# Local attention moved beside later projections, and the second score product over 128 partitions

## The chip, the cores and the metric

The kernel runs on one core of one Trainium2 chip. Its time is the device time of one execution in microseconds (us); three runs of the kernel before gave 2787.1, 2791.96 and 2795.49, median 2791.96. The trace comes from a further, profiled execution. The engines are TensorE (PE: matrix products; PEld: its weight loads), VectorE (DVE), ScalarE (ACT), GpSimd (POOL) and SyncE (SP, which here issues most transfers).

## The reference

A network of three blocks on 512 tokens of width 1024. The change lies in the first two, which are called layer 0 and layer 1 here. Such a layer takes tokens `x` (512) and context `xc` (256), normalizes and modulates them, projects them with `w_in`, and mixes four branches of 256 columns:

```
h  = rms_norm(x, n1) * (1 + sc1) + sh1;   hc likewise        # mods = silu(c) @ ada_w + ada_b
a_b, a_c, a_h, b_v, b_g, c_q, c_k, c_v, d_q, d_k, d_v = split_proj(h @ w_in)
ya = a_b * dwconv(a_c * a_h, conv_a)                         # 3 taps
yb = silu(layer_norm(dwconv(b_v * sigmoid(b_g), conv_b) + bias))      # 31 taps
yc = window_attention(rope(c_q), rope(c_k), c_v, kc_c, vc_c, sink)    # +-128 tokens, and the context
yd = global_attention(rope(rms_norm(d_q)), rope(rms_norm(d_k)), d_v, kc_d, vc_d)   # all 512, and the context
x  = x + g1 * (concat(ya, yb, yc, yd) @ w_out)
x  = x + g2 * expert_choice_ffn(rms_norm(x, n2) ...)          # 16 experts
```

There are 4 query heads of 64 columns in each attention and 2 key heads. In layer 0 the context goes through all of this too, in layer 1 it gives keys and values alone. A third block (gated delta rule, dilated attention, a wide feed-forward) follows.

## The kernel before, in words

Activations lie transposed, 128 channels on the partitions and tokens along the free axis, so a projection of 128 columns of `w_in` is one *unit*: 8 blocks of weights, each multiplied three times (`dense`, L418). Weights and activations are split in a high and a low part of a fast 32-bit type; high by high, high by low and low by high give full precision. A product over the 512 tokens writes PSUM tile `px` (L462), one over the 256 context tokens a second tile of the same name (L464, `pc` in the code). A unit's weights come by a transfer into one of five `raw` tiles, ACT makes the high part `wh` (L438), POOL the low part `wl` (L439); the transfer is asked for three units ahead. After a unit its eviction `ev` reads `px`: for queries and keys it applies the rotation `rope` (DVE L664, L666, L667 and POOL L665) and splits the result in high and low parts (L643 to L647), which small POOL transfers copy into the other half of the partitions.

The two long convolutions of layer 0 and 1 (`conv31`, L760) are 31 DVE instructions per 128 channels, one per tap, each adding into the same tile (L769, L772).

Attention (`att_gen`, `attend` L526) goes through *items*: one block of 128 queries and one pair of heads. A head's scores are one or two `s` tiles (own block with neighbours or all 512 tokens; the context). Each `s` tile is made of two products (L542): the query tile holds its high part on 64 partitions and its low part on the other 64, and meets the high part of the keys on both halves; the second product takes the 64 high query partitions alone and the low part of the keys. Then come the maximum (DVE L495 or L499), the exponential (ACT L510), the scaling by the sum (DVE L522, L523), transposes on PE (`pt`, L554), their copies (`PT`, ACT L557 for one head and DVE L559 for the other), and the product with the values (`y`, L572). There are two `s` tiles, one `pt`, one `y`, and one tile `misc` that modulation, head norms and convolution statistics share.

`ada_gen` makes the modulation: 16 of its blocks (L315, L324) run in layer 0 beside this work, each with four transfers of 512 KB into the same `raw` tiles.

What is interleaved with what is written in three `run_all` calls in program order, each a weave of generators with weights: (1) the units of branch b and 8 modulation steps; (2) the units of c and d, 16 modulation steps and all of `conv31`; (3) the six units of branch a, all of attention, and the rest of the modulation. In layer 1, which has no modulation to make, queries of c and d stand between the units of b already, and the long convolution starts after the eighth unit. Within this order a list scheduler of the framework may move an instruction ahead of others; each engine then runs its own list in order.

Of the kernel before, what the change touches and what calls it, by code (L numbers as in the profile page):

```python
# [134 lines left out]
def main_kernel(ctx, tc, I, out, stop=None, dbg=None, manual=False):  # L135
# [132 lines left out]
    for j in range(2):  # L268
        pre0[j] = raw_tile().rearrange("p (k c) -> p k c", k=8)
        SY.dma_start(pre0[j], I["w_in"][0, :, 1024 + 128 * j:1152 + 128 * j].rearrange("(k p) c -> p k c", p=128))  # L270
# [67 lines left out]
    if True:  # L338
# [79 lines left out]
        def dense(units, hh, hl, dw, dps, la=3, pre={}):  # L418
# [23 lines left out]
            for i in range(la):  # L442
                load(i)
            split(0)
            fresh = True
            for i, u in enumerate(units):
                ev, nt = u[1], u[2]
                k0, nk = u[3:5] if len(u) > 3 else (0, 8)
                load(i + la)
# [76 lines left out]
        def attend(ap, aps, groups, pw=768):  # L526
# [19 lines left out]
            def turn(i, g):  # L546
# [3 lines left out]
                for a in range(0, nt, 4):  # L550
# [4 lines left out]
                    pb = ap.tile([128, 512], F32, name="PT", bufs=4 if pw > 512 else 3)  # L555
# [34 lines left out]
        def layer(l):  # L590
# [6 lines left out]
            with (es_l0 if has else ExitStack()) as es, ExitStack() as er:  # L597
# [3 lines left out]
                sqp = pool(es, "sqp", 5)  # L601
# [20 lines left out]
                kC = dp.tile([128, 3, 768], F32R)  # L622
                kD = dp.tile([128, 3, 768], F32R)
# [10 lines left out]
                nrq = dp.tile([128, 2, 6, 2], F32)  # L634

# [13 lines left out]
                def put_q(dst, j, o, n, src, scale=None):  # L649
                    c = slice(o, o + n)  # L650
                    t = sqp.tile([128, 512], F32R, name="ql", bufs=2)
# [4 lines left out]
                def put_k(dst, o, n, src, scale=None):  # L656
                    c = slice(o, o + n)
                    split_to(dst[H0, 0, c], dst[H1, 1, c], dst[H0, 2, c], dst[H1, 2, c], src, scale)
                    G.dma_start(dst[H1, 0, c], dst[H0, 0, c])
                    G.dma_start(dst[H0, 1, c], dst[H1, 1, c])  # L660
# [197 lines left out]
                def qunit(n, ev, j):  # L858
                    return (colload2(w_in, c0[n] + 64 * j, c0[n] + 128 + 64 * j), ev, NT)

                u_kv = [unit("c_k", ev_rope(partial(put_k, kC)), 768), unit("d_k", ev_dk, 768),
                        unit("c_v", ev_v(vC), 768), unit("d_v", ev_v(vD), 768)]
                u_q = [qunit("c_q", ev_rope(partial(put_q, qC, j)), j) for j in range(2)] + \
                      [qunit("d_q", ev_dq(j), j) for j in range(2)]
# [4 lines left out]
                def terms(qt, kt, kv, g, n, a, b):  # L869
                    pr = slice(64 * kv, 64 * kv + 64)  # L870
                    q = qt[:, g, kv, n * 128:(n + 1) * 128]
                    return [(q, kt[:, kv, a:b]), (q[pr, :], kt[pr, 2, a:b])]

                def att_gen():
                    groups = []
                    for kv in range(2):
# [36 lines left out]
                        groups.append((hs, tuple(range(4)), yT[:, 6 + kv, 0:512], 512))  # L913
                        if has:
                            groups.append((hs, (4, 5), yT[:, 6 + kv, 512:768], 256))
# [963 lines left out]
```

## Time and profile before

| | |
|---|---|
| median of three runs | 2791.96 us |
| profiled execution, its own time | 2776.78 us |
| its span in the trace | 2774.0 us |
| PE busy | 2585.3 us, 93% |
| DVE, ACT, POOL busy | 1178.4, 876.3, 590.1 us |
| mean granted clock of PE | 0.974 |

Times in the trace count from the start of the span. Layer 0's projections and attention stand from 48 to 438 us, its output projection to 502, its experts to 1164; layer 1's from 1164 to 1439, output projection to 1470, experts to 1990; the third block fills the rest. A stretch in which PE is busy nearly throughout is bound by PE, and there only less work or shorter work on PE helps; one in which it is not is read by what ended its waits.

### The profile page before, as it was taken

What the parts mean: (1) busy time and instruction counts of PE and PEld (TensorE: products, weight loads), DVE (VectorE), ACT (ScalarE), POOL (GpSimd) and SP (SyncE); (2) the same over time, 40 slices, a digit from 0 to 9 for tenths busy, and PEclk for the clock granted to TensorE, in tenths of its full rate; (3) what the DMA queues carried; (4) which work ended last, traced back from release to release, by engine and by line L of the source; (5) the groups of instructions that cost most, each with busy time, mean ns of one, the idle gap of its engine ahead of it and who ended that gap; (6) DMA issues with size and microseconds to landing.
All of it is one profiled execution on the core that took longest, in us unless ns stands there. A gap on an engine that the chain in (4) does not pass through costs nothing.

```text
span 2774.0 us, 41538 instructions
## 1 busy us (share of the span) xinstructions
PE 2585.3 (93%) x16527; PEld 1530.4 (55%) x16527; DVE 1178.4 (42%) x2466; ACT 876.3 (32%) x1812; POOL 590.1 (21%) x495
## 2 busy tenths in 40 slices
PE   7989999799999999888997998889899999999998
PEld 3556677434444444466664321223377787888876
DVE  4684574412323233587653110212375555444411
ACT  4225443211111211334442211111354425444422
POOL 3243002000000000273111000000233232444443
PEclk9999999899999999899998999999899999999999
DMA  8655206599998988231047999999721102333331
GB/s 286 221 165 160 77 24 225 175 344 399 341 389 321 387 314 341 65 80 54 24 153 282 391 400 398 400 399 409 259 63 47 31 16 61 92 99 99 92 87 65
DMA packets 318327, 570.99 MB, mean 206 GB/s; under 512 B 36320, under 2 KB 187415, under 8 KB 317495
## 3 DMA queue, kind: packets, MB, share of 16 engines
q1 hardware_dynamic: 311143, 552.01, 55.4%
q0 software_dynamic: 6848, 16.27, 2.4%
q8 instruction: 130, 2.13, 0.3%
q14 instruction: 62, 0.51, 0.1%
q10 hardware_dynamic: 144, 0.08, 0.0%
HBM read 553.60 MB, written 10.49 MB: 203 GB/s over the span
## 4 chain that ended last, share of the span: by engine, by line
PE 70%; DMA 13%; DVE 8%; issue 1%; ACT 1%; POOL 1%; SPq 0%; ACTq 0%; DVEq 0%; POOLq 0%
PE px L462 19%; PE ax L1200 4%; PE ux L1200 4%; PE yx L1200 4%; PE s L542 3%; DMA rawA<-in_w_down_dram 3%; DVE yT L772 3%; PE y L572 3%; PE px L464 2%; PE g L462 2%; PE pt L554 2%; PE ac L1205 2%; PE tr L1313 2%; PE uc L1205 2%; PE yc L1205 2%; DMA rawA<-in_w_up_dram 2%
## 5 line engine op out<-in xcount | busy, mean ns | idle before, releaser
L439 POOL TENSOR_TENSOR wl<-raw,wh 128x512 fp32r<-128x512 f32 (+1 forms) x312 | 406.1, 1304 | 1046.1 <-ACT wh L438 755.3
L438 ACT ACTIVATE wh<-raw 128x512 fp32r<-128x512 f32 (+1 forms) x312 | 193.4, 625 | 469.5 <-PE px L462 209.7
L462 PE MATMUL px<-hh,wh 128*128 128x512 f32 x768 | 315.0, 412 | 8.0 <-DVE xT L1316 1.8
L462 PE MATMUL px<-hh,wl 128*128 128x512 f32 x768 | 315.9, 412 | 4.1 <-POOL wl L439 4.1
L462 PE MATMUL px<-hl,wh 128*128 128x512 f32 x768 | 315.6, 411 | 2.2 <-DVE hl L1004 1.9
L1284 DVE SCALAR_TENSOR_TENSOR Yx<-yx,gcol,Yx 64x512 fp32r<-64x512 f32 x64 | 48.0, 750 | 502.2 <-ACT Yx L1283 502.2
L1166 POOL DMA_INDIRECT xg<-hd,gidx x32 | 29.2, 914 | 845.6 <-PE tr L1178 787.3
L462 PEld LDWEIGHTS px<-hh,wh 128*128 128x128 f32 x768 | 148.2, 193 | 51.3 <-issue 12.4
L462 PEld LDWEIGHTS px<-hl,wh 128*128 128x128 f32 x768 | 148.4, 193 | 41.6 <-issue 11.3
L462 PEld LDWEIGHTS px<-hh,wl 128*128 128x128 f32 x768 | 148.8, 194 | 40.7 <-POOL wl L439 6.9
L1182 ACT ACTIVATE xt<-tr,mod,a 128x64 f32<-128x64 f32 x256 | 86.1, 405 | 197.3 <-PE tr L1178 193.2
L772 DVE SCALAR_TENSOR_TENSOR yT<-ub,cols,yT 128x512 f32<-128x512 f32 (+1 forms) x180 | 147.2, 862 | 1.2
L1283 ACT ACTIVATE Yx<-yx,gcol 64x512 fp32r<-64x512 f32 x64 | 43.6, 682 | 318.6 <-PE yx L1200 158.6
L1228 ACT ACTIVATE sa<-ax 128x512 f32<-128x512 f32 x32 | 19.1, 597 | 353.6 <-PE ax L1200 240.5
L1200 PE MATMUL ax<-rawA,xt 128*32 128x512 f32 x856 | 122.3, 603 | 0.0
L1200 PE MATMUL ux<-rawA,xt 128*32 128x512 f32 x800 | 119.2, 595 | 0.0
L1194 PE MATMUL ux<-rawA,xt 128*64 128x512 f32 x328 | 87.3, 611 | 7.7 <-DMA rawA<-in_w_up_dram 7.4
L1194 PE MATMUL yx<-rawA,hT 128*64 128x512 f32 x316 | 81.5, 621 | 13.0 <-DMA rawA<-in_w_down_dram 12.1
L1313 PE MATMUL tr<-oh,Yx 128*128 128x512 f32 x256 | 79.9, 440 | 11.3 <-ACT Yx L1283 8.1
L554 PE MATMUL pt<-tab,P 128*128 128x128 f32 x448 | 87.0, 289 | 3.0 <-ACT PT L557 1.5
L1194 PE MATMUL ax<-rawA,xt 128*64 128x512 f32 x316 | 77.3, 610 | 6.9 <-DMA rawA<-in_w_gate_dram 6.4
L464 PE MATMUL px<-hh,wh 128*128 128x256 f32 x240 | 73.2, 305 | 7.0 <-ACT sq L673 7.0
(573 smaller groups left out, 4907.5 us busy)
## 6 DMA issues: line engine op xcount, KB each, us to landing
rawA<-in_w_gate_dram SPq DMA_DIRECT2D x186, 512.0 KB, 9.4
rawA<-in_w_up_dram SPq DMA_DIRECT2D x182, 512.0 KB, 10.2
rawA<-in_w_down_dram SPq DMA_DIRECT2D x151, 512.0 KB, 10.4
raw<-in_ada_w_dram SPq DMA_DIRECT2D x80, 512.0 KB, 4.9
raw<-in_w_down_dram SPq DMA_DIRECT2D x74, 512.0 KB, 7.3
raw<-in_w_gate_dram SPq DMA_DIRECT2D x62, 512.0 KB, 10.1
raw<-in_w_in_dram SPq DMA_DIRECT2D x56, 512.0 KB, 4.9
raw<-in_w_up_dram SPq DMA_DIRECT2D x55, 512.0 KB, 6.5
```

The source lines that it names most:

```text
L438: A.activation(wh[:, :n], raw[i][:, a:a + n], AF.Copy)
L439: G.tensor_tensor(wl[:, :n], raw[i][:, a:a + n], wh[:, :n].bitcast(F32), op=OP.subtract)
L462: T.matmul(px, lhsT=w[:, k % 4, :], rhs=h[:, k0 + k, 0:512], start=st, stop=sp_)
L464: T.matmul(pc, lhsT=w[:, k % 4, :], rhs=h[:, k0 + k, 512:nt], start=st, stop=sp_)
L542: T.matmul(s[:, :w], lhsT=q, rhs=k, start=(a == 0), stop=(a == len(mm) - 1))
L554: T.transpose(pt[:, (t - a) * 128:(t - a + 1) * 128], P[:, t * 128:(t + 1) * 128], ident)
L772: V.scalar_tensor_tensor(acc[:, j, o:o + n], src, w, acc[:, j, o:o + n], op0=OP.mult, op1=OP.add)
L1182: A.activation(xt[:, kk, 0:64], p[:, k * NX:k * NX + 64], AF.Identity, bias=M[l][:, 24 + kk, 0:1], scale=a2[:, kk, 0:1])
L1194: T.matmul(px[64 * g:64 * g + 64, :], lhsT=lx(u), rhs=w[:, 512 * hf:512 * hf + 512], start=first, stop=last)
L1200: T.matmul(px[32 * g:32 * g + 32, :], lhsT=lx(u)[:, 32 * (g % 2):32 * (g % 2) + 32], rhs=w[:, 512 * hf:512 * hf + 512], start=first, stop= ...
L1205: T.matmul(pc[32 * g:32 * g + 32, :], lhsT=lc(u), rhs=w[:, 256 * q:256 * q + 256], start=first, stop=last)
L1313: T.matmul(p, lhsT=Y["x", pr][:, hl_, hf, c * 128:(c + 1) * 128], rhs=ohs[pr][hf], start=(n == 0), stop=(n == 2 * len(prs) - 1))
```

## The change

1. Each score tile's second product reads all 128 partitions: the keys' tile gets a fourth plane, so that the low parts of a key head lie on both halves too, and the whole query tile meets them (L542 is L553 afterwards). The small transfers after a key's split carry two planes each. The low query part loses its own two buffers and lies in a tile of the shared group `sq` until it is copied.
2. The units come as c, b, d, a in place of b, (c and d), a. The attention's items come as all of c, then all of d.
3. There are four weaves in place of three: the units of c alone; those of b with 28 of the 120 attention steps (18 of 80 in layer 1) and 8 modulation steps; those of d with as many and a part of `conv31` (16 of 42 steps, 8 of 21 in layer 1); those of a with the rest of all.
4. In layer 0 four units' weights are asked for at first, and after that the next unit's alone (`ahead=4`). The first two units' weights, loaded at entry, are now those of `c_k` and the first `c_q`.
5. The transposed probabilities use one group of tiles for the first 512 columns (`PT`) and another for the rest (`PU`), two buffers each, in place of four of one. `sqp` has 7 buffers in layer 1, 5 in layer 0 as before.

```diff
-        def dense(units, hh, hl, dw, dps, la=3, pre={}):
+        def dense(units, hh, hl, dw, dps, la=3, pre={}, ahead=None):
...
-                load(i + la)
+                load_to(i + la + 1 if ahead is None or i + la < ahead else max(ahead, i + 2))
                 split(i + 1)
...
-                    pb = ap.tile([128, 512], F32, name="PT", bufs=4 if pw > 512 else 3)
+                    pb = ap.tile([128, 512 if a == 0 else pw - 512], F32, name="PT" if a == 0 else "PU",
+                                 bufs=2 if pw > 512 else 3)
...
-                sqp = pool(es, "sqp", 5)
+                sqp = pool(es, "sqp", 5 if has else 7)
...
-                kC = dp.tile([128, 3, 768], F32R)
-                kD = dp.tile([128, 3, 768], F32R)
+                kC = dp.tile([128, 4, 768], F32R)
+                kD = dp.tile([128, 4, 768], F32R)
...
-                    t = sqp.tile([128, 512], F32R, name="ql", bufs=2)
+                    t = sqp.tile([128, 512], F32, name="sq")
...
                 def put_k(dst, o, n, src, scale=None):
                     c = slice(o, o + n)
-                    split_to(dst[H0, 0, c], dst[H1, 1, c], dst[H0, 2, c], dst[H1, 2, c], src, scale)
-                    G.dma_start(dst[H1, 0, c], dst[H0, 0, c])
-                    G.dma_start(dst[H0, 1, c], dst[H1, 1, c])
+                    split_to(dst[H0, 0, c], dst[H1, 1, c], dst[H0, 2, c], dst[H1, 3, c], src, scale)
+                    G.dma_start(dst[H1, 0:4:2, c], dst[H0, 0:4:2, c])
+                    G.dma_start(dst[H0, 1:4:2, c], dst[H1, 1:4:2, c])
...
                 def terms(qt, kt, kv, g, n, a, b):
-                    pr = slice(64 * kv, 64 * kv + 64)
                     q = qt[:, g, kv, n * 128:(n + 1) * 128]
-                    return [(q, kt[:, kv, a:b]), (q[pr, :], kt[pr, 2, a:b])]
+                    return [(q, kt[:, kv, a:b]), (q, kt[:, 2 + kv, a:b])]
...
-                mix = [u for p in zip(u_b, u_q) for u in p]
-                gd = dense((u_b + u_kv + u_q if has else mix + u_kv) + u_a, hh, hl, dw, psp, pre=pre0 if has else {})
-                n1 = 4 if has else 8
-                run_all((dense_part(gd, n1 * 3), n1 * 3), (steps(ga, 8), 8))
-                run_all((dense_part(gd, (12 - n1) * 3), 36 - n1 * 3), (steps(ga, 16), 16), (conv31(), 42 if has else 21))
-                run_all((gd, 18), (att_gen(), 120 if has else 80), (ga, 20))
+                gd = dense(u_c + u_b + u_d + u_a, hh, hl, dw, psp, pre=pre0 if has else {}, ahead=4 if has else None)
+                at, cv = att_gen(), conv31()
+                w1, w2, w3 = (28, 28, 64) if has else (18, 18, 44)
+                run_all((dense_part(gd, 12), 12))
+                run_all((dense_part(gd, 12), 12), (steps(at, w1), w1), (steps(ga, 8), 8))
+                c1 = 16 if has else 8
+                run_all((dense_part(gd, 12), 12), (steps(at, w2), w2), (steps(ga, 8), 8), (steps(cv, c1), c1))
+                run_all((gd, 18), (at, w3), (ga, 16), (cv, (42 if has else 21) - c1))
```

How the order on the engines moves is shown at three places. First PE's list in layer 1, at the second transposes of the key norm of d (`misc<-tab,sq`, L709 before and L722 after). Before:

```order
L464 MATMUL px<-hh,wl 128x256
L462 MATMUL px<-hh,wh 128x512
L709 MATMUL misc<-tab,sq 128x128 x2
L464 MATMUL px<-hh,wh 128x256
L462 MATMUL px<-hl,wh 128x512
L464 MATMUL px<-hl,wh 128x256
```

And at the same transposes in the changed kernel, where `s`, `pt` and `y` are attention's:

```order
L473 MATMUL px<-hh,wl 128x512
L722 MATMUL misc<-tab,sq 128x128 x2
L473 MATMUL px<-hh,wh 128x512
L473 MATMUL px<-hl,wh 128x512
L473 MATMUL px<-hh,wl 128x512
L553 MATMUL s<-kC,qC 128x384 x2
L553 MATMUL s<-kC,qC 128x256 x2
L565 MATMUL pt<-tab,P 128x128 x4
L584 MATMUL y<-PT,vC 64x128
L473 MATMUL px<-hh,wh 128x512
```

The window attention now stands between the products of the projections of d; before, none stood there, and all of it came after them.

Second DVE's list in layer 1, in the key norm of d (L698 to L710), where the taps of the long convolution (L772, L785 afterwards) stand. Before:

```order
L772 SCALAR_TENSOR_TENSOR yT<-ub,cols,yT 128x512 x11
L698 RECIPROCAL hr<-hsd 128x12
L772 SCALAR_TENSOR_TENSOR yT<-ub,cols,yT 128x512
L705 COPY sq<-hr 128x512
L772 SCALAR_TENSOR_TENSOR yT<-ub,cols,yT 128x512 x3
L710 TENSOR_TENSOR sq<-sq,misc 128x512
```

After, a piece of the list with taps and the steps of the softmax (L506 to L534):

```order
L782 TENSOR_SCALAR yT<-ub,cols 128x512
L785 SCALAR_TENSOR_TENSOR yT<-ub,cols,yT 128x512 x2
L525 SCALAR_TENSOR_TENSOR sms<-sms 128x1
L785 SCALAR_TENSOR_TENSOR yT<-ub,cols,yT 128x512
L533 RECIPROCAL sms<-sms 128x1
L506 ISA P,sms<-s,tabl 128x256
L506 ISA sms 128x1
L534 TENSOR_SCALAR P<-P,sms 128x512
L510 TENSOR_REDUCE sms<-s 128x1
L785 SCALAR_TENSOR_TENSOR yT<-ub,cols,yT 128x512
```

The runs of taps are shorter, and between them stand softmax steps, for which PE's next score tile waits.

Third ACT's list in layer 0, at the sigmoid of branch b (L748, L750; L761, L763 afterwards), where tables of functions are loaded. Before:

```order
L438 ACTIVATE wh<-raw 128x512
L750 ACT_TABLE_LOAD
L750 ACTIVATE yT<-px 128x256
L748 ACTIVATE yT<-px 128x512
L438 ACTIVATE wh<-raw 128x512 x2
L320 ACTIVATE sq<-misc 128x512
```

After:

```order
L521 ACTIVATE P,sms<-s,sms 128x256
L761 ACT_TABLE_LOAD
L761 ACTIVATE yT<-px 128x512
L763 ACTIVATE yT<-px 128x256
L442 ACTIVATE wh<-raw 128x512
L569 ACTIVATE PT<-pt 128x512
L518 ACT_TABLE_LOAD
L518 ACTIVATE sms<-sinkb,sms 128x1
L521 ACTIVATE P,sms<-P,sms 128x384
```

The exponential of attention now stands on both sides of the sigmoid, so its table is loaded again behind each. In the whole list of ACT there are 53 table loads before and 72 after.

## Rows read from the trace of the kernel before

**Rows 1.** The page: span, busy time and share, chain by line, transfers of `w_in`

```profile
span 2774.0 us, 41538 instructions
PE 2585.3 (93%) x16527; PEld 1530.4 (55%) x16527; DVE 1178.4 (42%) x2466; ACT 876.3 (32%) x1812; POOL 590.1 (21%) x495
...
raw<-in_w_in_dram SPq DMA_DIRECT2D x56, 512.0 KB, 4.9
```

**Rows 2.** Busy time by stretch (columns in the first line)

```profile
core 0: us, PE busy (x) PEld busy (x) DVE busy (x) ACT busy (x) POOL busy (x), PEclk, DMA share, GB/s
48.00:107.00 59.00, 55.00 (x267) 33.47 (x266) 28.84 (x52) 18.19 (x31) 20.39 (x17) 0.97 0.68 223
107.00:232.00 125.00, 110.72 (x606) 76.69 (x604) 96.81 (x168) 37.99 (x67) 52.19 (x49) 0.97 0.58 168
232.00:438.00 206.00, 205.48 (x1230) 133.40 (x1228) 128.79 (x397) 97.82 (x266) 28.52 (x26) 0.99 0.27 82
...
1164.00:1202.00 38.00, 36.25 (x145) 28.21 (x145) 27.13 (x42) 19.75 (x36) 21.79 (x18) 0.93 0.36 90
1202.00:1278.00 76.00, 58.75 (x280) 47.88 (x279) 73.06 (x87) 21.09 (x39) 51.56 (x43) 0.87 0.27 68
1278.00:1439.00 161.00, 155.54 (x897) 104.69 (x897) 104.45 (x294) 81.08 (x213) 22.39 (x18) 0.99 0.13 43
```

**Rows 3.** Chain that ended last, 1199 to 1285 us (start, us, what)

```profile
by line: DVE yT L772 67.4%; issue 5.6%; PE px L462 4.3%; DVE sq L667 3.1%; DVE sq L666 2.5%; DVE sq L664 2.5%; POOL sq L665 2.4%; DVE yT L769 2.3%; PE px L464 2.0%; PE misc L709 1.5%; DVE nrq L719 1.4%; DVE rq L718 1.4%; PE misc L781 1.3%; 
...
1201.26 1.68 DVE yT L772
...
1244.34 11.38 DVE yT L772 x11
```

**Rows 4.** PE's instructions in order (start, us, ...); score pairs and projections

```profile
293.16 1.43 PE L542 MATMUL s<-kD,qD 128*128 128x512 f32 x4
294.53 0.44 PE L554 MATMUL pt<-tab,P 128*128 128x128 f32 x2
...
355.11 0.59 PE L542 MATMUL s<-kC,qC 128*128 128x256 f32 x2
355.62 0.39 PE L464 MATMUL px<-hh,wh 128*128 128x256 f32 x1
...
357.42 0.39 PE L462 MATMUL px<-hh,wl 128*128 128x512 f32 x1
357.65 0.28 PE L464 MATMUL px<-hh,wl 128*128 128x256 f32 x1
357.77 0.70 PE L542 MATMUL s<-kC,qC 128*128 128x384 f32 x2
358.40 0.65 PE L554 MATMUL pt<-tab,P 128*128 128x128 f32 x4
```

**Rows 5.** PE's weight loads in order, the same stretch; idle time in brackets

```profile
357.65 0.19 PEld L542 LDWEIGHTS s<-kC,qC 128*128 128x128 f32 x1
358.03 0.18 PEld L542 LDWEIGHTS s<-kC,qC 64*128 64x128 f32 x1 [0.19 <-issue]
358.40 0.42 PEld L554 LDWEIGHTS pt<-tab,P 128*128 128x128 f32 x4 [0.19 <-issue]
```

**Rows 6.** The instructions of L542: duration min/median/max, shapes and counts

```profile
L542 PE MATMUL s<-kC,qC x144: 275/381/681, 229.9 to 1389.8; 128*128 128x256 f32 x56, 64*128 64x256 f32 x56, 128*128 128x384 f32 x16, 64*128 64x384 f32 x16
L542 PE MATMUL s<-kD,qD x144: 275/385/792, 293.2 to 1426.0; 128*128 128x256 f32 x40, 64*128 64x256 f32 x40, 128*128 128x512 f32 x32, 64*128 64x512 f32 x32
```

**Rows 7.** The taps of L772: duration min/median/max, shapes and counts

```profile
L772 DVE SCALAR_TENSOR_TENSOR yT<-ub,cols,yT x180: 464/739/1860, 95.6 to 1282.6; 128x512 f32<-128x512 f32 x120, 128x256 f32<-128x256 f32 x60
```

**Rows 8.** Groups of ACT, 232 to 438 us: busy, mean ns, idle before

```profile
L507 ACT ACT_TABLE_LOAD x2 | 2.6, 1283 | 0.0
```

**Rows 9.** Transfers of L654 (a query's low part), issue to landing

```profile
DMA to landing us min/median/max: 1.9/2.8/7.3
```

More of the change, by code (lines that the diff above doesn't have):

```diff
@@ L267, in main_kernel @@
     pre0 = {}
-    for j in range(2):
-        pre0[j] = raw_tile().rearrange("p (k c) -> p k c", k=8)
-        SY.dma_start(pre0[j], I["w_in"][0, :, 1024 + 128 * j:1152 + 128 * j].rearrange("(k p) c -> p k c", p=128))
+    pre0[0] = raw_tile().rearrange("p (k c) -> p k c", k=8)
+    SY.dma_start(pre0[0], I["w_in"][0, :, 1536:1664].rearrange("(k p) c -> p k c", p=128))
+    pre0[1] = raw_tile().rearrange("p (k c) -> p k c", k=8)
+    for h in range(2):
+        SY.dma_start(pre0[1][:, :, 64 * h:64 * h + 64],
+                     I["w_in"][0, :, 1280 + 128 * h:1344 + 128 * h].rearrange("(k p) c -> p k c", p=128))
     ada_load(0, 3, ada0[:, 3])
@@ L440, in split, with load_to @@
                         hi[i].append((wh, wl))
-            for i in range(la):
-                load(i)
+            loaded = 0
+            def load_to(n):
+                nonlocal loaded
+                while loaded < n:
+                    load(loaded)
+                    loaded += 1
+            load_to(la)
             split(0)
@@ L859, in qunit @@
                     return (colload2(w_in, c0[n] + 64 * j, c0[n] + 128 + 64 * j), ev, NT)
[L861 to L864, printed above, removed]
+                u_c = [unit("c_k", ev_rope(partial(put_k, kC)), 768)] + \
+                      [qunit("c_q", ev_rope(partial(put_q, qC, j)), j) for j in range(2)] + [unit("c_v", ev_v(vC), 768)]
+                u_d = [unit("d_k", ev_dk, 768)] + [qunit("d_q", ev_dq(j), j) for j in range(2)] + \
+                      [unit("d_v", ev_v(vD), 768)]
                 u_b = [unit("b_g", ev_bg(j), j=j) for j in range(2)] + [unit("b_v", ev_bv(j), j=j) for j in range(2)]
@@ L869, in terms @@
                 def terms(qt, kt, kv, g, n, a, b):
-                    pr = slice(64 * kv, 64 * kv + 64)
                     q = qt[:, g, kv, n * 128:(n + 1) * 128]
-                    return [(q, kt[:, kv, a:b]), (q[pr, :], kt[pr, 2, a:b])]
+                    return [(q, kt[:, kv, a:b]), (q, kt[:, 2 + kv, a:b])]
                 def att_gen():
-                    groups = []
+                    groups, late = [], []
                     for kv in range(2):
@@ L912, in att_gen @@
                                            nscale=lambda n, kv=kv, g=g: nrq[:, g, n, kv:kv + 1], sink=None, nsink=None))
-                        groups.append((hs, tuple(range(4)), yT[:, 6 + kv, 0:512], 512))
+                        late.append((hs, tuple(range(4)), yT[:, 6 + kv, 0:512], 512))
                         if has:
-                            groups.append((hs, (4, 5), yT[:, 6 + kv, 512:768], 256))
-                    yield from attend(ap, psp, groups)
+                            late.append((hs, (4, 5), yT[:, 6 + kv, 512:768], 256))
+                    yield from attend(ap, psp, groups + late)
                 def rest():
```

## The prediction

> **What bounds the kernel now.** I read the page first, then the busy time by stretch over the two layers' mixing, then the chain of waits in the stretch where PE is least busy, then PE's instructions one by one where attention runs. On the page PE is busy 93% of the span and DVE, the next, 42% [rows 1]: what is worth anything has to shorten PE's work or close PE's gaps. The stretches show which of the two holds where [rows 2]. In layer 0 from 48 to 232 us and in layer 1 from 1202 to 1278 us PE has gaps; in the attention stretches (232 to 438, 1278 to 1439) it has nearly none, and DVE is busy only 63 and 65% there. So each layer has two unlike parts: one where DVE decides, followed by one where PE decides. In the first the chain of waits says why: between 1199 and 1285 us two thirds of it are the taps of the long convolution, in one run of 11 for 11.38 us [rows 3], and a projection's eviction or a head norm stands behind them on DVE. In the second PE's list is attention and projections, and there I looked at what one matmul costs from start to start, since durations overlap.
>
> Those starts are the main finding. A projection product of 512 columns is followed by the next after 357.65 - 357.42 = 0.23 us, one of 256 columns after 357.77 - 357.65 = 0.12 us [rows 4]. A pair of score products of 256 columns takes 355.62 - 355.11 = 0.51 us, where two at 0.12 would be 0.24; a pair of 384 takes 358.40 - 357.77 = 0.63 us, where I estimate 2 x 0.175 = 0.35 between the two sizes; two pairs, of 512 and of 256, take 294.53 - 293.16 = 1.37 us, where 0.70 would do [rows 4]. The weight loads show where the rest goes: the first one, over 128 partitions, is done ahead of time, the 64-partition one starts only 0.38 us after it with 0.19 us of idle time that nothing else explains, and the load behind it, again over 128 partitions, has the same 0.19 us [rows 5].
>
> **The change, part by part.** *The second product over 128 partitions.* A pair becomes two products of the shape that projections have. If that is the cause, a 256 pair gains 0.27 us, a 384 pair 0.28, a 512 and a 256 pair together 0.67. By the counts there are 144 pairs: 96 of 256, 16 of 384, 32 of 512 [rows 6]. 32 of the 256 pairs go with the 512 ones: 32 x 0.67 = 21.4; the other 64 x 0.27 = 17.3; 16 x 0.28 = 4.5; together 43 us. All of it lies on PE in the stretches in which PE is bound. It could be less by what remains at the end of a pair, when transposes or a value product follow; the low end is half, 21, since half of the excess stands behind the 64-partition product. I take 43, since the rows show both halves.
>
> The Trainium skill ("TensorE: Matmul & The Clock Gate", section LDWEIGHTS) states that a weight load over 32 partitions takes as long as one over 128, and its closing table says the same of a small-K matmul by itself. The durations here agree (0.18 and 0.19 us) [rows 5], the starts do not: by that rule the 43 us would be 0. The change from one shape to the other is what its table has no line for.
>
> *The wider key planes.* `put_k` keeps its two transfers with twice the bytes, ACT and POOL split as much as before: 0. The low query part now takes one of the five `sq` tiles until its copy has landed, 2.8 us at the median [rows 9]; a query eviction then holds four of five. If the next of the four query evictions in layer 0 waits for that in full, it is 4 x 2.8 = 11 us; at the other end nothing, or a gain where the two buffers of before were the shortage. I take 0: a unit of 24 products of each size lasts 24 x 0.35 = 8.4 us, longer than the landing.
>
> *The long convolution among attention.* This closes gaps of PE. In layer 0 the stretch from 107 to 232 has 125 - 110.7 = 14.3 us of them, in layer 1 that from 1202 to 1278 has 76 - 58.75 = 17.3 [rows 2], together 31.6. PE then gets attention's products to fill them with, and the order shows that it does. DVE's own work is also less there: the taps have a median of 0.74 us but a largest of 1.86 [rows 7], and single ones in the chain take 1.68 [rows 3] while POOL is busy 51.6 of 76 us [rows 2]. The taps of the last weave meet a POOL that only splits weights, so DVE should not become longer. The cover for this is that PE's work stays above DVE's. In layer 0 DVE has 28.8 + 96.8 + 128.8 = 254 us in 390, PE 371 less 24 (80 of the 144 pairs are layer 0's); in layer 1 DVE 204.6 and PE 250.5 less 19 [rows 2]. So PE still leads in both, by 90 and by 27 us; in layer 1 it is close. The granted clock of 0.87 there [rows 2] says that part of PE's work ran at the lower level of 1.2 GHz after gaps; were it all at 2.4 GHz, up to 13% of 76 us = 10 us would come back. I take none of it, since part lies in gaps already counted.
>
> *What it adds.* ACT gets 19 more table loads of 1.283 us [rows 8], 24 us. They lie on an engine that is busy 97.8 of 206 us [rows 2], but each stands between scores and their exponential, and PE has only two score tiles. At one end they are all covered (0), at the other all on the path (24); I take the half, 12, by ACT's half-busy time. The shallower request for weights in layer 0 would cost at most 14 units x 4.9 us = 69 if a transfer [rows 1] were never covered, and nothing if always; with one unit asked for when the one before it begins, and units of at least 8.4 us, I take 0. The first weave of layer 0 loses its modulation, and with it its modulation transfers; what it loses there stands again in later weaves: 0. Split `PT` and `PU` tiles give each head as many as before: 0. Evictions of c in the first weave bring POOL work (rotation, splitting, 12 small transfers) beside the weight splits; POOL was busy 20.4 of 59 us there [rows 2], so 0.
>
> The sum: 43 + 14.3 + 17.3 - 12 = 62.6 us less. Made against the profiled execution, 2776.8 - 63 = 2714. The median of the runs shown lies 15 us above that execution, so the same difference from it gives 2792 - 63 = 2729 us.
>
> **The rivals.** *Shape does not matter.* If the excess of a pair comes from something that the change leaves alone (the switch to a new score tile, the same weights twice), 43 falls away: 31.6 - 12 = 20 us less, 2772. For it speaks that the loads themselves take equally long; against it that the idle time stands at exactly the two loads where the shape changes [rows 5], while projections switch tiles without it [rows 4]. The rule of the Trainium skill's TensorE page named above gives this outcome.
>
> *DVE takes over in the last weave.* With taps and softmax on one list, a score tile's maximum waits behind a run of taps, and PE with it. If the gaps of the two stretches are only moved, the 31.6 us stay: 43 - 12 = 31 less, 2761. Layer 1, with its 27 us of difference between the engines, is where it would be; for it speaks DVE's 73 of 76 us today [rows 2], against it that the runs of taps become shorter in the order.
>
> *All of it goes well.* No table load is felt and the clock comes back too: 43 + 31.6 + 10 = 85 less, 2707.
>
> *Slower: lock step through two score tiles.* Each of the 144 pairs needs its maximum before PE may write the pair after the next. If on average each waits for one tap behind POOL's use (1.68 us [rows 3]) in place of none, that is 144 x 1.68 = 242 us, less 74.6 gained: 2792 + 167 = 2959. It decides from 74.6 / 144 = 0.52 us a pair. A table load in front of every fourth exponential as well would add to it. Against it: today's pairs wait on DVE's side for PE, not the reverse, and PE's list has projections between pairs, so a short wait is filled. A milder form, 0.7 us a pair, gives 100 - 75 = 26 slower, 2818.
>
> That the change doesn't do what it says I leave out: the order shows attention among the units of b and d.
>
> **How the numbers follow.** Forecast (with the neighbours up to 15 us off) 0.50; all goes well 0.14; DVE takes over 0.18; shape does not matter 0.10; slower 0.08. Faster by over 0.3% (8 us, about what a measurement of this kernel can tell from no change, since its three runs lie 8.4 us apart) takes in the first three and nearly all of the fourth: 0.89; within 0.3% 0.04, slower 0.07. The range leaves out the slower rival and the far ends of the first two: 2695 to 2772. Its upper end is the outcome in which the shape is worth nothing, its lower end goes a little past the case in which all goes well, for a gain at the clock in layer 0 as well.
>
> **What would show it.** In the changed kernel's trace a pair of 256 should take about 0.24 us from start to start, of 512 about 0.46, no load of L553 should have 64 partitions, and the "issue" idle time at these loads should be gone. The attention stretches should be shorter by PE's work, with PE still without gaps. Taps should appear all over the second half of each layer with a mean near 0.74 us for 512 columns. PE's gaps in the former convolution stretches should be gone, and PE's clock near 1.0 there. ACT should show 19 more table loads in the two layers. Layer 0 should end its attention some 35 us earlier, layer 1 take some 30 us less from first projection to output projection; the experts and the third block should be as long as before. I would be wrong if pairs keep their 0.5 us, if PE waits for DVE's maxima over some 10 us in a layer, or if layer 0's first weave stalls on `sq` tiles or weights.

## The result, and the profile after

The changed kernel takes 2694.65 us (median of four runs, 2689.85 to 2696.23) against 2792.29 for the kernel before beside it: a ratio of 0.9649, 95% interval 0.963 to 0.9668. Two later comparisons gave 0.9682 (0.965 to 0.9715) and 0.9648 (0.9634 to 0.9661). The forecast was 2729, so the gain of some 95 us (98, and 86 and 100 by the medians of the later two) was half as large again as the 63 forecast, and 2694.65 lies just outside the range, by 0.35 us. Since the kernel before varies more than the changed one (its medians beside the runs of this study went from 2779 to 2792), I profiled both again; rows below named "before" are of that second execution (span 2784.5 us), and those of the changed kernel too (2692.0 us; its first had 2692.1).

The page of the changed kernel, for [rows 1]: TensorE has 77 us less to do than in the first profile of before, and is still what bounds the kernel.

```profile
span 2692.0 us, 41575 instructions
PE 2508.4 (93%) x16527; PEld 1523.7 (57%) x16527; DVE 1159.8 (43%) x2466; ACT 900.6 (33%) x1831; POOL 589.6 (22%) x495
```

To see where the time went, I cut from each trace the same work: from a layer's first projection to the last unit of its output projection, first layer 0, then layer 1. Before:

```profile
core 0: us, PE busy (x) PEld busy (x) DVE busy (x) ACT busy (x) POOL busy (x), PEclk, DMA share, GB/s
47.10:496.70 449.60, 430.73 (x2420) 291.69 (x2421) 271.87 (x649) 168.86 (x390) 116.76 (x104) 0.98 0.46 146
1165.20:1473.60 308.40, 286.31 (x1423) 207.31 (x1424) 212.76 (x430) 130.83 (x300) 109.46 (x87) 0.91 0.26 83
```

After:

```profile
46.90:445.80 398.90, 381.90 (x2420) 291.18 (x2421) 268.30 (x649) 181.25 (x401) 120.72 (x104) 0.96 0.54 167
1109.90:1378.50 268.60, 249.82 (x1423) 194.10 (x1424) 198.87 (x430) 141.66 (x308) 104.25 (x87) 0.95 0.31 98
```

PE has the same number of instructions in both, so this is like against like: 758.0 us became 667.5, 90.5 less, and the spans differ by 92.5. TensorE's gaps (length less PE busy) went from 41.0 to 35.8 only; its busy time fell by 85. I sorted that busy time by the starts of PE's instructions: score products went from 96.5 to 53.8 us (43 less, as forecast), modulation's products in layer 0 from 54.7 to 34.7 (20 less, not forecast), everything else by 23, of which 16 in layer 1, where the same instructions ran at a mean granted clock of 0.95 in place of 0.91. The other 7 are layer 0's, where the clock was not higher (0.96 after 0.98); what they are stays open.

How much of this is gaps and clock depends on the execution. In the first execution of before the same work took 746.4 us:

```profile
47.70:494.00 446.30, 427.48 (x2420) 289.79 (x2421) 271.65 (x649) 168.78 (x390) 116.62 (x104) 0.98 0.47 147
1163.70:1463.80 300.10, 275.40 (x1423) 199.32 (x1424) 213.61 (x430) 130.48 (x300) 108.89 (x87) 0.95 0.27 85
```

Layer 1 alone is 8.3 us shorter there, of the 10.5 us between the two spans. Between the first executions of the two kernels the difference is 80 us: 39 of score products, 19 of modulation, 8 of gaps and 13 of everything else, 5 of these in layer 1. So the first two terms hold in either pair, and the last one does not.

The score pairs answer to [rows 4]: a pair of 256 takes 255.06 - 254.82 = 0.24 us (0.51 before), two pairs of 512 and 256 take 259.24 - 258.36 = 0.88 (1.37 before). PE in order (start, us, what):

```profile
254.82 0.40 PE L553 MATMUL s<-kD,qD 128*128 128x256 f32 x2
255.06 0.39 PE L473 MATMUL px<-hh,wl 128*128 128x512 f32 x1
...
258.36 0.95 PE L553 MATMUL s<-kD,qD 128*128 128x512 f32 x4
259.24 1.04 PE L318 MATMUL misc<-raw,s 128*32 128x512 f32 x2
```

No load with 64 rows is left in layers 0 and 1 [rows 5, 6], and the taps are as forecast for their median, 0.739 us, but not their largest [rows 7]:

```profile
L553 PEld LDWEIGHTS s<-kC,qC x144: 186/189/338, 99.5 to 1247.6; 128*128 128x128 f32 x144
L553 PEld LDWEIGHTS s<-kD,qD x144: 186/188/245, 249.9 to 1330.1; 128*128 128x128 f32 x144
```

```profile
L785 DVE SCALAR_TENSOR_TENSOR yT<-ub,cols,yT x180: 457/739/1846, 145.0 to 1294.3; 128x512 f32<-128x512 f32 x120, 128x256 f32<-128x256 f32 x60
```

By weave, for [rows 2] (columns as above; layer 0's weaves of c, b, d, a, then layer 1's):

```profile
46.90:94.40 47.50, 40.37 (x192) 32.68 (x193) 29.05 (x42) 21.42 (x38) 37.05 (x36) 0.89 0.55 145
94.40:158.20 63.80, 63.15 (x437) 47.86 (x436) 37.74 (x121) 31.42 (x80) 13.65 (x11) 1.00 0.48 157
158.20:242.00 83.80, 75.52 (x482) 57.25 (x481) 73.39 (x177) 42.47 (x102) 34.31 (x32) 0.92 0.60 160
242.00:391.90 149.90, 148.95 (x1008) 108.64 (x1007) 115.02 (x289) 72.72 (x160) 20.19 (x15) 0.98 0.47 155
1109.90:1149.80 39.90, 34.13 (x144) 27.09 (x145) 27.58 (x44) 17.05 (x31) 23.63 (x21) 0.82 0.31 79
1149.80:1188.50 38.70, 35.71 (x204) 27.84 (x203) 25.68 (x76) 26.47 (x64) 14.30 (x13) 1.00 0.28 69
1188.50:1244.60 56.10, 51.26 (x310) 41.72 (x308) 53.24 (x113) 29.61 (x69) 30.00 (x28) 0.91 0.27 67
1244.60:1360.80 116.20, 111.02 (x698) 83.66 (x696) 88.10 (x195) 63.53 (x140) 28.88 (x22) 1.00 0.24 82
```

The gaps stand in other places than before: in the weaves of c (7.1 and 5.8 us) and of d (8.3 and 4.8), where the mean granted clock is 0.82 to 0.92, so part of the time at the lower of its two levels; besides, layer 1 has 3.0 and 5.2 in the weaves of b and a.

What the prediction did not see shows in modulation's pieces. One matmul has two records here, so x4 is two matmuls, x12 six, x16 eight. Before: two matmuls take 119.74 - 118.76 = 0.98 us, and six take 126.52 - 124.67 = 1.85:

```profile
118.76 1.05 PE L315 MATMUL misc<-raw,s 128*32 128x512 f32 x4 [1.20 <-DMA raw<-in_ada_w_dram]
119.74 0.39 PE L464 MATMUL px<-hh,wl 128*128 128x256 f32 x1
...
124.67 1.91 PE L315 MATMUL misc<-raw,s 128*32 128x512 f32 x12
126.52 0.50 PE L462 MATMUL px<-hh,wh 128*128 128x512 f32 x1
```

After: eight take 118.05 - 116.20 = 1.85 as well, and four take 296.07 - 295.08 = 0.99.

```profile
116.20 1.92 PE L318 MATMUL misc<-raw,s 128*32 128x512 f32 x16
118.05 0.66 PE L565 MATMUL pt<-tab,P 128*128 128x128 f32 x4
...
295.08 1.07 PE L318 MATMUL misc<-raw,s 128*32 128x512 f32 x8
296.07 0.66 PE L565 MATMUL pt<-tab,P 128*128 128x128 f32 x4
```

Four such matmuls, which write four different groups of 32 partitions, cost as much together as two do. Before, modulation's order on PE had mostly pieces of two, or six and two; after, mostly of eight. At 0.98 us for a piece of up to four and 1.85 for one of five to eight, the pieces in the two orders sum to 53.9 and 34.6 us, which is what the traces have (54.7 and 34.7).

Modulation also held part of the gaps that the prediction put down to VectorE. In the first execution of before, this is what PE waited for from 107 to 232 us, the stretch with 14.3 us of gaps [rows 2] (us in total, times, longest):

```profile
PE misc L315 <- DMA raw<-in_ada_w_dram: 7.7, 5, 3.2
PE misc L689 <- DVE mod L326: 3.7, 1, 3.7
PE misc L735 <- DVE mod L326: 1.7, 1, 1.7
```

More than half of the 14.3 us ended with the landing of modulation's weights, the rest mostly with VectorE's sums for modulation. In layer 0 of the changed kernel no wait of PE ended with such a landing.

### The profile page after: what moved, and what is told of

The parts are those of the page before. It is cut to its first block, busy times and chain, and to the rows that moved or that the text cites. A ratio compares the mean times of both kernels' runs of the same rounds, so it can differ in the third digit from the quotient of the medians.

```text
span 2692.1 us, 41575 instructions
## 1 busy us (share of the span) xinstructions
PE 2512.2 (93%) x16527; PEld 1526.5 (57%) x16527; DVE 1156.3 (43%) x2466; ACT 900.7 (33%) x1831; POOL 590.2 (22%) x495
## 4 chain that ended last, share of the span: by engine, by line
PE 69%; DMA 15%; DVE 9%; POOL 2%; issue 2%; ACT 2%; SPq 1%; ACTq 0%; DVEq 0%; POOLq 0%
PE px L473 20%; PE ux L1215 4%; PE ax L1215 4%; PE yx L1215 4%; DMA rawA<-in_w_down_dram 3%; PE g L473 2%; PE y L584 2%; PE tr L1328 2%; PE s L553 2%; PE ac L1220 2%; PE px L475 2%; PE uc L1220 2%; PE yc L1220 2%; DMA rawA<-in_w_up_dram 2%; PE ux L1209 2%
## 5 line engine op out<-in xcount | busy, mean ns | idle before, releaser
L785 DVE SCALAR_TENSOR_TENSOR yT<-ub,cols,yT 128x512 f32<-128x512 f32 (+1 forms) x180 | 126.6, 720 | 0.6
L1328 PEld LDWEIGHTS tr<-oh,Yx 128*128 128x128 f32 x256 | 45.7, 196 | 60.4 <-DVE xT L1331 23.6
## 6 DMA issues: line engine op xcount, KB each, us to landing
raw<-in_w_gate_dram SPq DMA_DIRECT2D x62, 512.0 KB, 10.1
```

Of the source, the lines that this page charges most:

```text
L785: V.scalar_tensor_tensor(acc[:, j, o:o + n], src, w, acc[:, j, o:o + n], op0=OP.mult, op1=OP.add)
L1328: T.matmul(p, lhsT=Y["x", pr][:, hl_, hf, c * 128:(c + 1) * 128], rhs=ohs[pr][hf], start=(n == 0), stop=(n == 2 * len(prs) - 1))
```

## The experiments

My theory after the result: the second product is worth what was forecast; the late request for weights joins modulation's pieces; the new order closes gaps and, with them, brings the clock back. The rivals: the shorter scores come of the new order, pieces of the new weaves, and the order's gain is the spread of the taps alone. Variants of the changed kernel are compared with its 2693.9, though some ran on other chips (its own three medians lie within 3 us); variants of the kernel before are compared with the kernel before beside them, by the ratio.

**Both kernels again.** No edit.

> The kernel before, unchanged, profiled once more. The forecast carried over the 15.2 us by which its first profiled execution (2776.78) lay below the median of its timed runs (2791.96). If that was chance in one execution, this profile comes out near 2792 and the change's gain between traces is near 98 us, like that between the timed runs; if a profiled execution of this kernel is always faster, it comes out near 2777 again.

Measured: 2787.8 (ten runs, 2774.1 to 2804.9), the profiled execution 2786.5.

> The changed kernel, unchanged, beside its variants. Timed near 2694.7 us again. If the profiled execution of any kernel is about 15 us below its timed runs, this one comes out near 2680; the first one was 2693.99, so I expect 2694.

Measured: 2693.9, profiled 2693.87. So the profiled executions lie among the timed ones: the 15 us that the forecast carried over were the kernel before's own spread, over 30 us wide, against 4 to 6 for the changed one.

**The second product, undone and done alone.**

```diff
-                    return [(q, kt[:, kv, a:b]), (q, kt[:, 2 + kv, a:b])]
+                    pr = slice(64 * kv, 64 * kv + 64)
+                    return [(q, kt[:, kv, a:b]), (q[pr, :], kt[pr, 2 + kv, a:b])]
```

> The changed kernel with the second score product back on 64 partitions, and all else as changed. If the shape costs what the traces show (score products 50.5 us in layer 0 and 42.4 in layer 1 before, 29.6 and 24.3 after), it is 39 us slower than the changed kernel, near 2734; part may hide in gaps, so 25 to 45. If the shape does not matter and the shorter score time came with the new order, 0 to 5 us, near 2697.

Measured: 2735.2 (2733.0 to 2742.2), 41.3 slower than the changed kernel.

> The kernel before with the second score product over 128 partitions, and with the smaller tiles that make room for it (low query part in a shared tile, probabilities in two groups of tiles); units, weaves and requests as before. If the shape makes the gain, 39 us faster than the kernel before, near 2753 (the forecast's own term was 43). If the gain needs the new order, 0 to 5 us faster.

The edit: items 1 and 5 of the change put into the kernel before. Measured: 2747.4, ratio 0.9864 (0.9824 to 0.9903), 38 us. The shape makes it, from either side. The rule of the Trainium skill ("TensorE: Matmul & The Clock Gate", section LDWEIGHTS), that a load's time does not depend on its rows, agrees with the loads here (0.18 and 0.19 us), but it does not price a change from 128 to 64 rows and back, so the outcome of 0 that was drawn from it did not come. The variant's windows hold a second finding, beside those of before:

```profile
48.10:484.90 436.80, 406.56 (x2420) 289.03 (x2421) 269.05 (x649) 167.85 (x390) 131.99 (x104) 0.96 0.48 150
1153.40:1438.60 285.20, 256.01 (x1423) 196.66 (x1424) 213.88 (x430) 130.40 (x300) 110.25 (x87) 0.94 0.29 89
```

Busy time fell by 54 us, but the gaps rose from 41.0 to 59.4. In layer 0, 8 of the 11 us added are waits for modulation's weights (17.9 in place of 10.1), nearly all before attention begins, so the shorter score products do not explain them; the variant's smaller tiles and chance (this execution was the slowest of its four) are not told apart as causes.

**The request for weights.** In the changed kernel the deep request again, in the kernel before the late one alone:

```diff
-                gd = dense(u_c + u_b + u_d + u_a, hh, hl, dw, psp, pre=pre0 if has else {}, ahead=4 if has else None)
+                gd = dense(u_c + u_b + u_d + u_a, hh, hl, dw, psp, pre=pre0 if has else {})
```

> The changed kernel with the weights in layer 0 asked for three units ahead again, as before. In the traces a modulation piece of up to four matmuls takes 0.98 us and one of five to eight 1.85 us, since two matmuls fill only part of TensorE's columns; before, the blocks went as 2+6 or 2+2+2+2, afterwards mostly as 8. If the deep request causes the small pieces (it holds four of the five raw tiles, so a modulation block gets one at a time), the order here gives pieces worth 47.7 us in place of 34.6: 13 us slower, near 2707. If the grouping came with the new weaves, 0; if weights that come later cost waits, up to 5 us faster than the changed kernel.

Measured: 2708.6 (2702.2 to 2713.5), 14.7 slower than the changed kernel's 2693.9; modulation's products 48.1 us.

> The kernel before with the changed kernel's request for weights in layer 0 (four units at first, then one ahead), and nothing else. By the prices of pieces its modulation matmuls take 41.9 us in place of 53.9: 12 us faster than the kernel before, near 2770 if that is 2782. If small pieces cost nothing on the path, 0; if late weights stall the projections, slower by up to 10.

Measured: 2768.0, ratio 0.9941 (0.992 to 0.9962), 16 faster; modulation's products 46.5 us.

```profile
50.70:490.50 439.80, 421.74 (x2421) 291.98 (x2422) 272.32 (x649) 167.82 (x389) 126.56 (x104) 0.97 0.47 147
1154.80:1456.30 301.50, 277.80 (x1423) 201.31 (x1424) 213.29 (x430) 130.57 (x300) 109.15 (x87) 0.94 0.27 85
```

The first is as the pieces say (13.4 us of products). In the second the products give 8 of the 12 expected. Its layer 0 is 9.8 us shorter than in the second execution of before and 6.5 than in the first; the other 6.9 us lie in layer 1, where the edit changes nothing and PE's list is the same, so they are the spread of that kernel. So by the traces the request alone is worth 7 to 10 us there; the timed 16 has an interval of 11 to 22. PE's waits for modulation's weights in layer 0 follow the request too: 10.1 us before, 4.2 with the late request, none in the changed kernel, 5.5 with the deep one put back. My reading is that five `raw` tiles serve both streams, that units asked for three ahead hold most of them, and that a modulation block then gets its four transfers singly; no run changes the number of tiles, so that it is the tiles and not the order of the transfers is not shown.

**Both together, units and weaves as before.**

> The kernel before with the second score product over 128 partitions and the late request for weights in layer 0 together; units and weaves as before. If the two gains simply add (39 and 15 us measured alone), near 2729 where the kernel before is 2783, and the new order of units and weaves is then worth some 35 us to the changed kernel's 2694. The forecast's terms for the order gave 31.6 less 12, so 20 us, which would put this kernel near 2714.

Measured: 2729.3 (2727.8 to 2733.6). The gains add, and the order of units and weaves is worth 2729.3 - 2693.9 = 35 us. Its windows have 53.9 us of gaps (25.7 and 28.2), the changed kernel's 35.8:

```profile
47.60:470.10 422.50, 396.77 (x2421) 288.69 (x2422) 274.50 (x649) 167.26 (x389) 126.17 (x104) 0.97 0.51 157
1134.60:1419.20 284.60, 256.38 (x1423) 196.39 (x1424) 213.96 (x430) 130.34 (x300) 110.48 (x87) 0.95 0.29 89
```

**Taps left out, in both kernels.**

```diff
-                                else:
+                                elif t == 30:
```

> The changed kernel with 29 of the 31 taps of each long convolution left out, which takes about 122 us of work from VectorE. It has 17 us of TensorE gaps in layer 0 and 18 in layer 1. If the taps make those behind the first weave (8.3 in layer 0; 2.9, 5.1 and 5.1 in layer 1), some 18 us go, and the clock returns some more: 18 to 25 faster, near 2673. If the gaps are those of evictions and of softmax itself, 0 to 6 faster; the gaps of the first weaves (7 and 6 us, behind GpSimd) stay in either case.

Measured: 2669.2 (2668.2 to 2670.8), 24.7 faster than the changed kernel.

> The kernel before with the same taps left out. The forecast put 31.6 us of TensorE gaps down to them (14.3 in layer 0, 17.3 in layer 1). If that is right, 31 us go and some 10 more with the clock: near 2745 if the kernel before is 2782. If part of those gaps is the chain of evictions and weight splits, which stays, only 10 to 20 us go.

Measured: 2734.4 (2733.7 to 2738.4), ratio 0.9826 (0.9794 to 0.9858), 49 faster, and its four runs lie within 5 us. Before without its taps:

```profile
49.10:484.00 434.90, 427.73 (x2420) 291.01 (x2421) 195.26 (x533) 168.99 (x390) 113.24 (x104) 0.98 0.47 149
1149.30:1423.50 274.20, 266.77 (x1422) 193.43 (x1423) 152.69 (x372) 128.12 (x297) 100.51 (x87) 0.98 0.30 93
```

Gaps fell by 26.4 us, and busy time by 22.5 with the same instructions: the clock of layer 1 is 0.98 in place of 0.91. Against this execution of before a gap was paid nearly twice; against the first, with 0.95, gaps fell by 29 and busy time by 8. The changed kernel without its taps:

```profile
47.10:430.60 383.50, 370.64 (x2420) 283.44 (x2421) 204.09 (x533) 181.63 (x401) 115.75 (x104) 0.99 0.56 174
1097.70:1358.30 260.60, 245.74 (x1423) 193.61 (x1424) 155.73 (x372) 144.71 (x310) 102.54 (x87) 0.96 0.33 101
```

That is 23 us less (8 of gaps, 15 of busy time). The time came as expected, but not by the road named: 18 us of gaps were to go. By the timed runs the change took away half of what the taps cost.

**Where in the order it lies.** All of attention in the last weave, all else as changed:

```diff
-                run_all((dense_part(gd, 12), 12), (steps(at, w1), w1), (steps(ga, 8), 8))
+                run_all((dense_part(gd, 12), 12), (steps(ga, 8), 8))
...
-                run_all((gd, 18), (at, w3), (ga, 16), (cv, (42 if has else 21) - c1))
+                run_all((gd, 18), (at, 120 if has else 80), (ga, 16), (cv, (42 if has else 21) - c1))
```

> The changed kernel with its units, requests and long convolution as they are, but all of attention in the last weave, as in the kernel before. If window attention in the second and third weaves is what closes the gaps, the gaps of the order-unchanged variant come back: it had 25.7 and 28.0 us where the changed kernel has 17.0 and 18.1, so some 18 us slower, near 2712; a part may be kept by taps that stand in the last weave. If it is the spread of the long convolution alone that helps, 0 to 5 slower. If attention's new place costs as much as it brings (table loads, waits on maxima), it is faster than 2694.

Measured: 2737.2 (2731.5 to 2743.6), 43 slower.

```profile
47.40:470.80 423.40, 396.61 (x2421) 297.05 (x2422) 260.05 (x649) 177.50 (x397) 123.49 (x104) 0.95 0.50 158
1136.80:1424.20 287.40, 257.39 (x1422) 196.83 (x1423) 208.18 (x430) 132.42 (x300) 106.88 (x87) 0.94 0.29 88
```

Gaps 56.8 us, 21 more than in the changed kernel, and 22 more of busy time, of which 6 are modulation's. The gaps I expected; the busy time that comes with them I had missed a second time. With the taps spread but attention late, the kernel is no faster than with the old order of units and weaves (2729.3).

```diff
-                c1 = 16 if has else 8
+                c1 = 8 if has else 4
```

> The changed kernel with 8 (layer 0) and 4 (layer 1) steps of the long convolution in the third weave in place of 16 and 8, the rest in the last. In the stretch of the third weave VectorE is busy 53 of 56 us in layer 1, in the last 87 of 112. If VectorE's saturation in the third weave makes the gaps there (5 us in layer 1, 8 in layer 0), moving 16 taps (10 us) in layer 1 and 32 in layer 0 gains 4 to 10 us, near 2687. If the gaps move along with the taps, 0.

Measured: 2694.0 (2690.1 to 2697.2), no change. The third weave's gaps are 9.1 us in layer 0 (8.3 with more taps there) and 2.7 in layer 1 (4.8), those of both layers together 37.7 (35.8).

> The changed kernel with the units in the order b, c, d, a: the first weave has b alone, the second c with modulation and 16 of 42 taps' steps (8 of 21 in layer 1), the third d with window attention and 20 (10), the last the rest; so window attention comes one weave later. If the first weave's gaps come from c's evictions on GpSimd, they fall from 8.5 and 8.9 to some 4 and 3 us; against it the taps of the second weave meet those same evictions on GpSimd, and the last weave has 16 and 10 more steps of attention, which TensorE bounds anyway. Together 5 us faster to 8 slower than 2694; I take 0. If the first weave is what holds the kernel, 10 faster.

Measured: 2712.9 (2705.9 to 2721.2), 19 slower than the changed kernel, well past the 8 that I allowed. The first weaves' gaps did fall (2.5 and 0.8 us in place of 7.1 and 5.8), but those of the third, of d, rose from 8.3 and 4.8 to 14.5 and 13.4, and modulation's products from 34.7 to 42.7. Units, taps and attention move together in this edit, so the run does not say which of them costs it.

**Table loads.** `Sqrt`, `Sigmoid` and `Silu` of the mixing taken as `Copy` or `Identity`.

> The changed kernel with the roots, sigmoids and long-convolution silus of the two layers' mixing taken as plain copies (identity), so that ScalarE keeps the exponential's table: 32 of 34 table loads of 1.283 us in the mixing go, 41 us of ScalarE; nothing else is left out. The forecast took half of the loads' time as lying on the path (12 of 24 us for 19 loads). By that rule 32 loads are worth 20 us: near 2674. If other work covers them, 0 to 5 us faster, near 2692.

Measured: 2691.6 (2689.1 to 2694.9), 2 less than the changed kernel, inside its spread. In layer 0's stretch one group with one load is left, where the changed kernel has 19 in six groups:

```profile
L518 ACT ACT_TABLE_LOAD x1 | 1.3, 1283 | 0.0
```

So ScalarE had room for them, and little or nothing of the 12 us that the forecast took off was on the path.

**The first weave, and a faster version.** What PE waited for in layer 1's weave of c (us in total, times, longest):

```profile
PE px L473 <- POOL wl L443: 4.5, 1, 4.5
PE px L473 <- ACT hh L416: 1.2, 1, 1.2
PE px L473 <- DVE hl L417: 1.1, 2, 0.7
```

GpSimd's weight split stands behind the rotation, the splits and the small transfers of c's evictions. The first edit moves the rotation's product for c to VectorE, the second the low parts of c's splits too:

```diff
-                        put(0, 512, rope(q))
+                        put(0, 512, rope(q, V))
...
-                            G.tensor_tensor(lo, src[pr, :], h.bitcast(F32), op=OP.subtract)
+                            eng.tensor_tensor(lo, src[pr, :], h.bitcast(F32), op=OP.subtract)
```

> The changed kernel with the rotation's product with the sine on VectorE in place of GpSimd, for the three units of c alone. The first weaves have 8.5 and 8.9 us of TensorE gaps, and the chain there runs through GpSimd's weight splits, queued behind the rotation (1.3 to 1.9 us each) and the key and query splits. If that queue makes the gaps, three products of 1.3 us leave it in each layer: 4 to 8 us faster, near 2688. If VectorE, which finishes the norm there, becomes the one that is waited for, 0 to 3 slower.

Measured: 2689.9 (2687.7 to 2693.1), 4 faster, the ranges overlapping.

> The changed kernel with the rotation's product with the sine, and the low parts of the split of keys and queries that GpSimd computes, on VectorE for the units of c. The rotation alone gave 4 us. If GpSimd's queue still makes the rest of the first weaves' gaps, another 3 to 6 us go: near 2685. If VectorE is the next to be waited for, as much is lost: 2690 to 2694.

Measured: 2683.5 (2677.8 to 2689.2). Layer 1's first weave has 1.6 us of gaps in place of 5.8, with GpSimd busy 12 us in place of 24:

```profile
1105.90:1139.90 34.00, 32.39 (x145) 25.52 (x146) 32.60 (x50) 16.61 (x30) 12.28 (x13) 0.89 0.37 93
```

Beside the changed kernel on one chip, with a further variant:

> The changed kernel once more, on the same chip as the two that follow, for comparison: 2694 again, with a spread of some 5 us.

Measured: 2691.7 (2690.1 to 2695.4).

> The variant with c's rotation and splits on VectorE once more, beside the changed kernel on one chip: 2684 again, 10 less than the changed kernel, if the gain is real; if it was the chip, 2690 to 2694.

Measured: 2684.9 (2682.1 to 2687.4), 7 faster with no overlap: it beats both kernels, 0.9619 (0.9606 to 0.9633) of before.

```diff
-                w1, w2, w3 = (28, 28, 64) if has else (18, 18, 44)
+                w1, w2, w3 = (38, 18, 64) if has else (26, 10, 44)
```

> The same variant with 38 of the 56 early attention steps in the second weave and 18 in the third (26 and 10 in layer 1), in place of 28 and 28 (18 and 18). VectorE is busy 73 of 84 and 53 of 56 us in the third weaves, 37 of 64 and 27 of 41 in the second. If the third weaves are bound by VectorE's taps and softmax together, this takes some 7 us of softmax out of them in layer 0 and as much in layer 1 and gains 3 to 8 us: near 2679. If attention among the taps is what fills TensorE's gaps there, the gaps come back and it is 3 to 8 slower: near 2689. By the run with all attention late I hold the second for a little likelier.

Measured: 2685.8 (2679.5 to 2689.3): no difference that could be told, neither of the two outcomes named.

## Why the prediction was wrong

The direction and the largest term were right, the other terms not. Between the second executions the forecast's 62.6 us stand against 90.5. Second product 43 against 43, gaps 31.6 against 5, modulation's products 0 against 20, all other busy time 0 against 23, table loads 12 off against about nothing. The miss in the gaps, 26 us, offsets half of the other three: that the time came so near the range is partly luck. Point by point:

- *Second product, 43 us.* Right: 43 in the second executions, 39 in the first, 41 and 38 in the runs. Idle time at exactly the two loads with a change of shape [rows 5] was good evidence.
- *"The first weave of layer 0 loses its modulation ...; what it loses there stands again in later weaves: 0"*, and the shallower request between 69 us slower and nothing. This step failed: the time of a moved instruction was taken as fixed. Modulation's products cost 20 us less, because they come in pieces of eight; the request alone makes 13 of these in the changed kernel and 8 in the kernel before. The bound for the request had only a slower end; that a later request leaves tiles to somebody else was not asked. The pieces and their lengths could be counted beforehand, in the order and in the trace of before.
- *Gaps, 31.6 us.* This step failed too. All of it was put down to VectorE's taps, by a chain of waits read in layer 1 alone [rows 3], but 7.7 of layer 0's 14.3 us waited for modulation's weights, and these waits went with the request and the order. The gaps fell by 5 only (8 between the first executions): the weaves of c now have 7.1 and 5.8 us, part of it behind GpSimd, where the prediction said 0, and those of d 8.3 and 4.8. That PE's gaps hang on the taps did hold, in layer 0 indirectly: without taps the kernel before is 49 us faster, and its waits for modulation's weights are 4.8 us in place of 10.1.
- *The clock, 0 taken of 10.* Mis-sized, by an amount that the executions do not settle: everything else in layer 1 took 16 us less between the second ones and 5 between the first; leaving out the taps of before took 20 us of layer 1's busy time against the second and 9 against the first. The 10 had been worked out from one stretch of one execution. In the second execution of before layer 1 as a whole ran at 0.91, in the first at 0.95. Most of the difference between the two lies there, so much of that kernel's spread does.
- *Table loads, 12 us against.* Wrong: some 2 us at most can be told, and that for 32 loads.
- *The 15 us between profile and median.* Not an offset: the first profile of before was an ordinary execution among those from 2771 to 2805 us.

Of the rivals, "DVE takes over in the last weave" was right in small: taps still cost the changed kernel 23 to 25 us, and the gaps stand more in the weaves of d (13 us) than in the last ones (6). "All goes well" (2707) had the nearer terms for clock and table loads, but nothing for modulation. Lock step through the two score tiles did not come: the pairs cost what the shape says. What stays open is how much of the order's 35 us (39.6 between the traces) each cause is worth by itself: gaps are 18 of the 39.6, modulation's pieces 10, other busy time 11, but one brings the other, and no run separates them.

## What to carry to other kernels

Count a moved instruction again where it lands: modulation's 32-column matmuls cost by the piece (0.98 us for up to four, 1.85 for five to eight), not by the matmul, and how their weights are asked for makes the pieces. Before a gap is put down to the busiest engine beside it, read what ended it. And where TensorE has gaps, price the work that runs at the lower clock around them too; without the taps of the kernel before it came to 8 us beside 29 of gaps, or to 22 beside 26, by the execution.

## What I had not expected of the hardware

Two matmuls with 32 columns each, on two groups of 32 partitions, take 0.98 us, and eight on four groups 1.85. A load with 64 rows between loads with 128 costs some 0.27 us a pair of products, although each load takes 0.18 to 0.19 us. The same instructions of layer 1 took 286 us of TensorE's time at a mean granted clock of 0.91 and 275 at 0.95 in two executions of one kernel, and 267 at 0.98 without the taps.
